# One weight queue over all projection parts, half-row norm steps, and output weights split on GpSimd in a one-core hybrid encoder layer

## The chip, the core and the metric

The kernel runs on one core of a Trainium2 chip. That core has a matrix engine (TensorE, in the profile PE for matmuls and PEld for weight loads), VectorE (DVE), ScalarE (ACT), GpSimd (POOL) and SyncE (SP), which here only issues DMAs. Data move between the chip's memory (HBM) and the on-chip buffers by 16 DMA engines, which the queues of SP and ACT feed. The metric is the device time of one execution in microseconds (us), lower is better.

## The reference, cut to what matters

One layer is run for 2048 prompt rows and for 8 streams of 16 sample rows (128 rows together), width 1024, all in float32:

```
n = rmsnorm(x)
z, xbc, dt_raw, q, k, v, f_raw = split_columns(n @ w_in)
y_ssd = ssd_mixer(z, xbc, dt_raw, ...)        # causal conv 4, chunked state scan, gate silu(z), group norm
y_fox = fox attention(q, k, v, cumsum(logf))  # 8 heads of 64, per-head forget gates, causal
h = x + concat(y_ssd, y_fox) @ w_out
u = causal_dwconv(rmsnorm(h) @ w_up)          # width 3
y = rmsnorm(h + (silu(u_gate) * u_value) @ w_down)
```

The outputs are y for both groups and the new caches and states.

## The kernel before, in words

Every float32 operand of a matmul is split into a high part (rounded) and a low part (the rest), and each product is three matmuls: high by high, high by low, low by high. The high part is made by a copy on ACT, the low part by a subtraction on POOL or DVE (`split`, `split2`).

The prompt is cut into four parts of 512 rows. Part 0 also holds the 128 sample rows (tile `SMP`). For each part, `a_head(p)` makes the normalised, transposed rows `nT`: it loads the transposed rows `xT`, finds the size of each row (`sizes` by plain rows `xt` on ACT, two half rows of 512 for each of four tiles, one `xt` buffer; for part 0 `sizes_by_columns` by matmul with ones), turns the sizes into diagonals `dg`, and multiplies. `a_body(p)` then projects: first v with the gate columns, v's other half, q and k, and after a break (`yield None`) the convolved x/B/C columns and z. `proj_tm` and `proj_cm` load their weight tile `craw` (two buffers) and split it into `cmw` (three buffers) where they are called. `gates(p)` turns the gate columns into decays and cumulative sums.

Attention (`attention`, in two passes: `s_phase` finds row maxima, `t_phase` the weights and sums) runs over the parts in order. Between its tiles the code places steps of the next projections by a credit (`fill`), and steps of a side job by a count (`sides`): `sample_attention` in part 0, the 17 SSD chunks (`ssd_chunk`) in parts 1 to 3. At attention tile 216 of 320 `out_steps` begins: `out_weights` loads and splits the eight rows of `w_out`, then `out_proj` computes `h` tile by tile, which goes on after attention. Last comes the ConvFFN over three groups of rows (`ffn_part`), untouched here.

The order of TensorE's instructions is the written one:

```
with tc.manual_schedule(engines={nc.tensor.engine}):
```

On ACT, DVE, POOL and SP a planner sets the order: it runs the program against a simulated clock and issues on each engine what is ready there, earliest written first. Each of these engines then runs its list in that order, whatever the real times are. A tile with `bufs=n` has n places; a new one waits until the last use of the one n before it. Four queue names pick the issuer of DMAs: `DQ = "sass"` makes `dma`, `dS` and `dA` go to SP and `dW` to ACT. Only weights (`dW`) are issued from ACT.

Of the kernel before, what the change touches and what calls it, by code (L numbers as in the profile page):

```python
# [17 lines left out]
P = 128  # L18
# [48 lines left out]
def hybrid_step(ctx: ExitStack, tc: tile.TileContext, i: dict, o: dict):  # L67
# [91 lines left out]
    def a_head(p):  # L159
# [18 lines left out]
        def sizes_by_columns(n, xTs):  # L178

            sq = at([P, 2, 4, 256], "cmw", WA)  # L180
            for kk in range(2):
                S.activation(sq[:, kk, :, :n * P], xTs[kk][:, :, :n * P], AF.Square)
            pz = tpt()
            for c in range(n):
                for k in range(KT):
                    T.matmul(pz[:, c:c + 1], sq[:, k // 4, k % 4, c * P:(c + 1) * P], ones[:, 0:1], start=k == 0, stop=k == KT - 1)
            ss = at([P, 2], "ss", 4)
            V.tensor_scalar(ss[:, 0:n], pz[:, 0:n], 1.0 / D, EPS, op0=ALU.mult, op1=ALU.add)
            G.tensor_tensor(ss[:, 0:n], ss[:, 0:n], mhalf[:, 0:n], op=ALU.pow)
            return [ss[:, c:c + 1] for c in range(n)]  # L190

        def sizes(c):
            ss = at([P, 2], "ss", 4)
            for hf in range(2):
                xt = at([P, 512], "xt", XB)
                dA(xt, i["xr"][c][:, hf * 512:(hf + 1) * 512])
                S.activation(xt, xt, AF.Square, accum_out=ss[:, hf:hf + 1])
            V.tensor_add(ss[:, 0:1], ss[:, 0:1], ss[:, 1:2])
            rsq(ss[:, 0:1], D)
            return ss[:, 0:1]  # L200

        def diagonals(ss):
            dgs = []
            for x in ss:
                dg = at([P, P], "dg", 2)
                S.activation(dg, ident, AF.Identity, scale=x)
                dgs.append(dg)
            return dgs

        def rows(e, w, c0, n, col, xsrc, xTs, dgs):  # L210
# [15 lines left out]
            for kk in range(0, KT, 4):  # L226
                xT = xTs[kk // 4]
                for k in range(4):
                    V.scalar_tensor_tensor(xT[:, k, :N], xT[:, k, :N], g1c[:, kk + k:kk + k + 1], pr[:, :N],
                                           op0=ALU.mult, op1=ALU.mult)  # L230
                split(xT[:, :, :N], wt[:, 0, kk:kk + 4, col:col + N], wt[:, 1, kk:kk + 4, col:col + N], S,
                      V if kk else G)
                if not kk:
                    yield

        if first:
            for t in todo:
                xTs = load(*t)
                dgs = diagonals(sizes_by_columns(t[3], xTs))
                yield  # L240
                for _ in rows(*t, xTs, dgs):
                    pass
                yield
# [13 lines left out]
    def gates(p, dtf):  # L257
# [11 lines left out]
        S.activation(u, u, AF.Exp, scale=-1.0)  # L269

# [5 lines left out]
        for m in (15, 13, 11, 9, 7, 5, 3):  # L276
            V.scalar_tensor_tensor(ac, ac, 1.0 / m, z, op0=ALU.add, op1=ALU.mult)
        V.scalar_tensor_tensor(ac, ac, 1.0, s, op0=ALU.add, op1=ALU.mult)
# [8 lines left out]
        if p == 0:  # L287
            dS(o["logf"][:, SMP], lf[:, 4])
        yield
# [17 lines left out]

        yield
# [68 lines left out]

    def a_body(p):
# [4 lines left out]
        def proj_tm(src, n, use):  # L383
            wm = []
            for e in range(2):
                raw = at([P, 4, 272], "craw", 2)
                dW(raw[:, :, :n], src[:, 4 * e:4 * e + 4])
                we = at([P, 2, 4, 272], "cmw", WA, F32R)
                split2(raw[:, :, :n], we[:, 0, :, :n], we[:, 1, :, :n], G)
                wm.append(we)  # L390
            for w, wt in wins:
                for c in win_tiles(w):
# [10 lines left out]
                    yield 1.45  # L403

# [19 lines left out]

        yield from proj_tm(i["w_tm0"], 272, use_v(1))
        gs = gates(p, dtf)
        next(gs)
        yield from proj_tm(i["w_tm"][0], 256, use_v(0))

        def load_cm(ct):  # L430
            raw = at([P, 4 * 272], "craw", 2)
            dW(raw[:, 0:D], i["w_cm"][ct])
            wc = at([P, 2, KT, P], "cmw", WA, F32R)
            split2(raw[:, 0:D].rearrange("p (k c) -> p k c", c=P), wc[:, 0], wc[:, 1], G)
            return wc

        def proj_cm(ct, use, pad):
            wc = load_cm(ct)
            for w, wt in wins:
# [10 lines left out]
                yield W * 0.0055  # L450

# [70 lines left out]
    def ssd_chunk(c):  # L522
# [6 lines left out]
        dma(sg.rearrange("p h l -> p (h l)"), ac_d[c:c + 1].rearrange("c h p -> c (h p)").to_broadcast([P, D]))  # L529

# [257 lines left out]
    def sample_attention():  # L788
# [33 lines left out]
        for b in range(NB):  # L822
# [11 lines left out]
            for a in range(2):  # L834
                vt = bt_([P, 2, 528], "k12", KB)
                dma(vt[:, :, 0:512], i["cv"][b, a * 256:(a + 1) * 256].rearrange("(c p) d -> p c d", p=P))
                vc += [vt[:, 0], vt[:, 1]]
            ps = [pss(), pss()]
# [49 lines left out]
    wo = []  # L888

    def out_weights():  # L890
# [19 lines left out]
    def out_proj(c, after=None):  # L910
        mr = op.tile([P, KT, P], F32, tag="raw", name="raw", bufs=2)
        mx = op.tile([P, 2, KT, P], F32R, tag="mx", name="mx", bufs=2)

        for ks in ([slice(0, KT - 1), slice(KT - 1, KT)] if 12 <= c < 16 else [slice(0, KT)]):
            dA(mr[:, ks], mix_d[c][:, ks])
            split(mr[:, ks], mx[:, 0, ks], mx[:, 1, ks], S, V)
# [10 lines left out]
        with tc.issue_after(after) if after is not None else ExitStack():  # L927
# [4 lines left out]
            else:  # L932
                for e in range(2):
                    for k in range(KT):
                        part(e, k)
                        if k % 2:
                            yield 1.36
        for e in range(2):
# [234 lines left out]
    def part_steps(p):  # L1173
# [3 lines left out]
        for k, c in enumerate(body):  # L1177
            if c is None:
                break
            if k in (12, 40) and hd:  # L1180
                next(hd)
# [16 lines left out]
    def out_steps():  # L1198
# [3 lines left out]
        for c in [SMP] + list(range(11)):  # L1202
            yield from out_proj(c)
# [4 lines left out]
    def open_out():  # L1208
# [9 lines left out]
    with tc.manual_schedule(engines={nc.tensor.engine}):  # L1218
        bodies = [a_body(0)]

        for k, c in enumerate(bodies[0]):
            if c is None:
                break
            if k < 4:
                next(head0)
            if k == 12:
# [6 lines left out]
        for u in att:  # L1233
# [20 lines left out]
            while gen is not None and credit > 0 and not hold:  # L1254
                c = next(gen, None)
                if c is None:
# [134 lines left out]
```

## Time and profile before

| | |
|---|---|
| median of 3 runs | 3159.74 us (3157.91 to 3166.94) |
| profiled execution | 3159.18 us, span of its instructions 3157.5 us |
| busy share of the span | PE 96%, PEld 85%, DVE 57%, ACT 34%, POOL 27% |
| mean granted TensorE clock | 0.984 of full |
| chain that ended last | PE 85%, DMA 8%, DVE 2%, ACT 2% |

A row of waits reads "who <- what ended the wait: us in total, times, longest". In a row of the time line, the bracket holds the idle time of the engine before the instruction and what ended it. PEclk is the granted clock of TensorE, 1.00 at 2.4 GHz and 0.50 at 1.2 GHz. ACTq and SPq are DMA issues and other work of these engines' sequencers.

### The profile page before, as it was taken

Reading aid. Unit: us, or ns where it says so; the run is one execution under the profiler, and the core shown is the slowest. Engines: PE = TensorE matmul, PEld = TensorE weight load, DVE = VectorE, ACT = ScalarE, POOL = GpSimd, SP = SyncE. Lnnn points to the kernel's source line nnn. Section 1 sums busy time; section 2 is a strip of 40 time slices with the busy share of each in tenths; the row PEclk is TensorE's granted clock in tenths of the full one; section 3 lists DMA queues with packets and bytes.
Section 4 is the critical chain, followed back from the end, with each engine's and each line's share of the span. In section 5 each row is a group of like instructions: output and inputs, shape, how many; then the busy total and the mean of one; then the engine's idle time right before and its main releaser. Section 6 shows DMA issues by size and latency. Waiting matters only on the chain.

```text
span 3157.5 us, 45849 instructions
## 1 busy us (share of the span) xinstructions
PE 3039.0 (96%) x17888; PEld 2682.1 (85%) x17888; DVE 1788.8 (57%) x3294; ACT 1066.7 (34%) x1927; POOL 865.8 (27%) x654
## 2 busy tenths in 40 slices
PE   7988998899999998999999999999999999999998
PEld 7886877787788775777899999999999999999998
DVE  4264466647565654543455555566555556766666
ACT  3343344444444444332322232233222223332322
POOL 3322322222222212000233232333223232433332
PEclk9998999899999999999999999999999999999999
DMA  4856675575556546445522121232121122322221
GB/s 123 247 174 202 200 244 158 181 223 165 162 155 204 153 132 187 161 148 181 171 67 67 54 69 61 72 116 79 61 67 61 60 67 83 105 67 81 74 69 65
DMA packets 233137, 395.77 MB, mean 125 GB/s; under 512 B 62544, under 2 KB 118488, under 8 KB 232920
## 3 DMA queue, kind: packets, MB, share of 16 engines
q1 hardware_dynamic: 181224, 238.41, 24.3%
q10 hardware_dynamic: 51696, 154.43, 15.8%
q8 instruction: 141, 2.31, 0.3%
q14 instruction: 76, 0.62, 0.1%
HBM read 314.51 MB, written 78.25 MB: 124 GB/s over the span
## 4 chain that ended last, share of the span: by engine, by line
PE 85%; DMA 8%; DVE 2%; ACT 2%; issue 1%; SPq 1%; POOL 1%; ACTq 0%; DVEq 0%; POOLq 0%
PE mm L120 11%; PE mm L121 11%; PE mm L122 11%; PE pv L696 6%; PE dn L1025 5%; PE dn L1026 5%; PE dn L1027 5%; PE mm L444 3%; PE mm L445 3%; PE mm L446 3%; DMA xt<-in_xr 2%; PE dn L923 2%; PE dn L925 2%; PE dn L924 2%; PE mm L397 2%; PE mm L399 2%
## 5 line engine op out<-in xcount | busy, mean ns | idle before, releaser
L105 POOL TENSOR_TENSOR wr<-raw,wr 128x1024 fp32r<-128x1024 f32 x198 | 476.5, 2415 | 1032.5 <-ACT wr L102 1024.5
L120 PE MATMUL mm<-nT,wr 128*128 128x386 f32 (+1 forms) x2112 | 696.4, 330 | 1.3 <-ACT wr L102 0.8
L121 PE MATMUL mm<-nT,wr 128*128 128x386 f32 (+1 forms) x2112 | 695.3, 329 | 0.1
L122 PE MATMUL mm<-nT,wr 128*128 128x386 f32 (+1 forms) x2112 | 694.4, 329 | 0.0
L1003 DVE SCALAR_TENSOR_TENSOR ac<-mm,cw,ac 128x384 f32<-128x384 f32 (+1 forms) x528 | 301.6, 571 | 344.8 <-ACT ac L1001 337.1
L1001 ACT ACTIVATE ac<-mm,cw 128x384 f32<-128x384 f32 (+1 forms) x264 | 172.7, 654 | 784.6 <-PE mm L122 784.0
L1028 DVE TENSOR_TENSOR y<-y,dn 128x512 f32<-128x512 f32 x374 | 255.0, 684 | 267.4 <-PE dn L1027 264.6
L121 PEld LDWEIGHTS mm<-nT,wr 128*128 128x128 f32 x2112 | 399.3, 189 | 6.8 <-DVE nT L105 0.3
L120 PEld LDWEIGHTS mm<-nT,wr 128*128 128x128 f32 x2112 | 397.5, 188 | 7.7 <-ACT wr L102 1.1
L122 PEld LDWEIGHTS mm<-nT,wr 128*128 128x128 f32 x2112 | 397.9, 188 | 5.7
L112 POOL TENSOR_TENSOR cmw<-craw,cmw 128x512 fp32r<-128x512 f32 (+1 forms) x192 | 248.6, 1317 | 467.8 <-ACT cmw L109 348.1
L444 PE MATMUL mm<-nT,cmw 128*128 128x256 f32 (+2 forms) x1024 | 309.7, 302 | 12.7 <-DVE cac L489 8.6
L671 DVE TENSOR_REDUCE nm<-s 128x1 f32<-128x512 f32 (+2 forms) x320 | 192.9, 607 | 198.6 <-PE s L668 114.1
L445 PE MATMUL mm<-nT,cmw 128*128 128x256 f32 (+2 forms) x1024 | 299.0, 292 | 0.0
L446 PE MATMUL mm<-nT,cmw 128*128 128x256 f32 (+2 forms) x1024 | 299.0, 292 | 0.0
L1025 PE MATMUL dn<-wr,ht 128*128 128x512 f32 x748 | 294.4, 394 | 2.9 <-DVE y L1028 1.7
L696 PE MATMUL pv<-pr,v 128*128 128x512 f32 (+3 forms) x640 | 293.5, 549 | 0.5 <-issue 0.5
L1026 PE MATMUL dn<-wr,ht 128*128 128x512 f32 x748 | 292.7, 391 | 0.0
L1027 PE MATMUL dn<-wr,ht 128*128 128x512 f32 x748 | 290.1, 391 | 0.0
L102 ACT CAST wr<-raw 128x1024 fp32r<-128x1024 f32 x198 | 203.2, 1042 | 174.1 <-PE dn L1027 161.4
L733 ACT ACTIVATE pr<-s 128x512 f32<-128x512 f32 (+1 forms) x320 | 169.3, 531 | 237.3 <-PE s L729 173.2
L668 PE MATMUL s<-ks,q 68*128 68x512 f32 (+2 forms) x320 | 199.8, 630 | 20.0 <-ACT pr L733 11.2
(294 smaller groups left out, 5174.9 us busy)
## 6 DMA issues: line engine op xcount, KB each, us to landing
raw<-in_w_up ACTq DMA_DIRECT2D x132, 512.0 KB
raw<-in_w_down ACTq DMA_DIRECT2D x66, 512.0 KB
craw<-in_w_cm ACTq DMA_DIRECT2D x64, 512.0 KB
k<-k_d SPq DMA_DIRECT2D x80, 256.0 KB
craw<-in_w_tm ACTq DMA_DIRECT2D x24, 512.0 KB
q_d<-qk SPq DMA_DIRECT2D x96, 128.0 KB
k_d<-qk SPq DMA_DIRECT2D x96, 128.0 KB
ks<-k_d SPq DMA_DIRECT2D x80, 136.0 KB
```

The costliest lines, as they stand in the source:

```text
L105: leng.tensor_sub(lo, src, hi.bitcast(F32))
L120: T.matmul(ps[:, :W], whi(k), wt[:, 0, k, :W], start=k == 0, stop=False)
L121: T.matmul(ps[:, :W], whi(k), wt[:, 1, k, :W], start=False, stop=False)
L122: T.matmul(ps[:, :W], wlo(k), wt[:, 0, k, :W], start=False, stop=k == n - 1)
L444: T.matmul(ps[:, :W], wc[:, 0, k, :], wk[:, 0], start=k == 0, stop=False)
L445: T.matmul(ps[:, :W], wc[:, 0, k, :], wk[:, 1], start=False, stop=False)
L446: T.matmul(ps[:, :W], wc[:, 1, k, :], wk[:, 0], start=False, stop=k == KT - 1)
L696: m = T.matmul(pv[:, of:512], vr[:, jj], pr[:, :512 - of], start=first, stop=last)
L1003: V.scalar_tensor_tensor(ac[:, 0:n], ps[:, j:j + n], cw2[:, ct, j:j + 1], ac[:, 0:n], op0=ALU.mult, op1=ALU.add)
L1025: T.matmul(ps, ht[:, 0, ts_], wd[:, 0, cc], start=x == 0, stop=False)
L1026: T.matmul(ps, ht[:, 0, ts_], wd[:, 1, cc], start=False, stop=False)
L1027: T.matmul(ps, ht[:, 1, ts_], wd[:, 0, cc], start=False, stop=x == len(g) - 1)
```

## The change

- The weight tiles of all four parts stand in one list (`wq`). `wload` issues the next raw tile from SP instead of ACT; `pump`, called at each projection step, splits the next loaded tile if one of the three `cmw` places is free and keeps two raw tiles ahead; `need` hands the tiles to the projections. The first two tiles are loaded and split inside `a_head(0)`.
- The order of the projections becomes v(second half), q0, v(first half), k0, q1, k1 ..., and after the break x0, z0, x1, z1, x2 to x7.
- `a_head(p)` for p > 0 issues one half row a step (calls at steps 8, 10, ..., 24 instead of all at step 12). The `xt` buffer is still one. For part 0 the squares move from `cmw` to the `k12` places, and the diagonals and the low parts go to DVE.
- `gates` has four more breaks and is advanced at each projection step instead of each projection.
- `ssd_chunk` has two more steps after its loads, `sample_attention` one more after its loads of each stream; one chunk moves from part 1 to part 2 and one more to part 3.
- `out_weights` splits wholly on POOL, without the `issue_after`; `out_rows` issues the load of the next tile's rows a tile ahead and splits them late in the tile before; three attention tiles pass between the first such load and its use.

```diff
         def sizes_by_columns(n, xTs):
-            sq = at([P, 2, 4, 256], "cmw", WA)
+            sq = []
             for kk in range(2):
-                S.activation(sq[:, kk, :, :n * P], xTs[kk][:, :, :n * P], AF.Square)
+                sq.append(bt_([P, 4 * 264], "k12", KB)[:, 0:D].rearrange("p (k t) -> p k t", k=4))
+                S.activation(sq[kk][:, :, :n * P], xTs[kk][:, :, :n * P], AF.Square)
...
-        def sizes(c):
-            ss = at([P, 2], "ss", 4)
-            for hf in range(2):
-                xt = at([P, 512], "xt", XB)
-                dA(xt, i["xr"][c][:, hf * 512:(hf + 1) * 512])
-                S.activation(xt, xt, AF.Square, accum_out=ss[:, hf:hf + 1])
-            V.tensor_add(ss[:, 0:1], ss[:, 0:1], ss[:, 1:2])
-            rsq(ss[:, 0:1], D)
-            return ss[:, 0:1]
+        def half_row(n):
+            xt = at([P, 512], "xt", XB)
+            dma(xt, i["xr"][todo[0][2] + n // 2][:, n % 2 * 512:(n % 2 + 1) * 512])
+            return xt
...
-                S.activation(dg, ident, AF.Identity, scale=x)
+                if first:
+                    V.tensor_scalar_mul(dg, ident, x)
+                else:
+                    S.activation(dg, ident, AF.Identity, scale=x)
...
-                      V if kk else G)
+                      V if kk or first else G)
...
-        ss = [sizes(todo[0][2] + c) for c in range(4)]
-        yield
+        xt = half_row(0)
+        yield
+        ss = []
+        for n in range(8):
+            if n % 2 == 0:
+                x = at([P, 2], "ss", 4)
+            S.activation(xt, xt, AF.Square, accum_out=x[:, n % 2:n % 2 + 1])
+            if n < 7:
+                xt = half_row(n + 1)
+            if n % 2:
+                V.tensor_add(x[:, 0:1], x[:, 0:1], x[:, 1:2])
+                rsq(x[:, 0:1], D)
+                ss.append(x[:, 0:1])
+            yield
...
+    def wload():
+        src, n = wq[len(raws)]
+        raw = at([P, 4 * 272], "craw", 2)
...
+        dma(raw, src.rearrange("p (k c) -> p k c", c=P) if n is None else src)
+        raws.append(raw)
+
+    def pump():
+        if len(tiles) < len(raws) and len(tiles) - used[0] < WA:
+            wsplit()
+        while len(raws) < len(wq) and len(raws) - len(tiles) < 2:
+            wload()
...
-        for pair in range(4):
-            for ct, kind in ((pair, 0), (4 + pair, 1)):
-                next(gs, None)
-                yield from proj_cm(ct, use_qk(kind, pair), 0)
+        for c in rest():
+            next(gs, None)
+            yield c
...
-        for ct in range(8):
-            yield from proj_cm(8 + ct, use_x(ct), PAD1)
-        yield from proj_tm(i["w_tm"][1], 256, use_z(0))
-        yield from proj_tm(i["w_tm"][2], 256, use_z(1))
+        yield from proj_cm(use_x(0), PAD1)
+        yield from proj_tm(256, use_z(0))
+        yield from proj_cm(use_x(1), PAD1)
+        yield from proj_tm(256, use_z(1))
+        for ct in range(2, 8):
+            yield from proj_cm(use_x(ct), PAD1)
...
-            with tc.issue_after(exps[-1]):
-                split2(raws[k], w[:, 0], w[:, 1], G)
+            split(raws[k], w[:, 0], w[:, 1], G, G)
...
-        for c in [SMP] + list(range(11)):
-            yield from out_proj(c)
+        cs = [SMP] + list(range(11))
+        g = out_rows(cs[0])
+        next(g)
+        yield ("wait", 3)
+        mx = next(g)
...
-    sides = {0: (sample_attention, 5 * NB + 1), 1: (lambda: chunks(SMP, 0, 1, 2), 49), 2: (lambda: chunks(3, 4, 5, 6, 7), 51),
-             3: (lambda: chunks(*range(8, 16)), 81)}
+    sides = {0: (sample_attention, 6 * NB + 1), 1: (lambda: chunks(SMP, 0, 1), 45), 2: (lambda: chunks(2, 3, 4, 5, 6), 61),
+             3: (lambda: chunks(*range(7, 16)), 109)}
```

## Rows read from the trace of the kernel before

**Rows 1.** Busy time in stretches of the span: the stretch and its length, then for each engine its busy time and instructions, then PEclk, the DMA engines' busy share and GB/s. 0 to 60 is the start, 140 to 600 holds the changes from part 0 to 1 and from 1 to 2, 1160 to 1260 the turn to the output projection, 1310 to the end mainly the ConvFFN.
```profile
0.00:60.00 60.00, 40.77 (x229) 39.61 (x229) 25.45 (x73) 20.56 (x29) 22.64 (x30) 0.97 0.36 116
140.00:260.00 120.00, 106.50 (x797) 97.26 (x798) 63.62 (x186) 44.60 (x98) 32.60 (x33) 0.97 0.59 186
260.00:360.00 100.00, 82.01 (x584) 65.70 (x583) 51.91 (x136) 37.05 (x84) 28.71 (x29) 0.81 0.63 192
460.00:600.00 140.00, 122.68 (x767) 101.71 (x766) 88.98 (x178) 53.66 (x114) 37.31 (x37) 0.93 0.58 176
600.00:1160.00 560.00, 547.58 (x3667) 449.59 (x3666) 332.51 (x643) 247.37 (x528) 146.72 (x156) 0.99 0.57 170
1160.00:1260.00 100.00, 82.09 (x390) 56.73 (x389) 49.01 (x77) 40.69 (x79) 26.41 (x30) 0.91 0.61 180
1310.00:3158.00 1848.00, 1833.01 (x9813) 1676.88 (x9811) 1070.01 (x1748) 541.67 (x817) 513.52 (x284) 1.00 0.27 86
```

**Rows 2.** Waits of TensorE's matmuls from 0 to 1310 us: who, what ended the wait, us in total, times, longest.
```profile
PE s L570 <- ACT pr L733: 12.6, 2, 9.1
PE s L668 <- ACT pr L733: 10.9, 5, 5.1
PE mm L444 <- DVE cac L489: 8.6, 3, 5.0
PE s L588 <- DVE ss L198: 7.8, 1, 7.8
PE tp L225 <- ACT dg L206: 7.7, 2, 5.8
...
PE s L668 <- DMA q<-q_d: 5.6, 2, 4.2
...
PE s L728 <- ACT pr L733: 4.4, 3, 2.1
...
PE tp L345 <- DVE g_2k L331: 1.6, 1, 1.6
```

**Rows 3.** Waits of ACT from 0 to 1310 us, same columns.
```profile
ACT xt L197 <- DMA xt<-in_xr: 64.7, 21, 6.3
...
ACT sg L532 <- DMA sg<-ac_d: 32.6, 12, 5.7
...
ACT wo L109 <- DMA raw<-in_w_out: 13.7, 3, 6.4
...
ACT cmw L182 <- PE tp L186: 10.2, 1, 10.2
```

**Rows 4.** Time line of the turn to the output projection, ACT and then TensorE: start, length, engine, line, instruction, tiles, shape, count, and the idle time before it.
```profile
1180.42 1.04 ACT L109 CAST wo<-raw 128x1024 fp32r<-128x1024 f32 x1 [5.79 <-DMA raw<-in_w_out]
...
1230.82 1.04 ACT L109 CAST wo<-raw 128x1024 fp32r<-128x1024 f32 x1 [6.43 <-DMA raw<-in_w_out]
1236.57 1.04 ACT L102 CAST mx<-raw 128x1024 fp32r<-128x1024 f32 x1 [4.71 <-DMA raw<-mix_d]
...
1182.02 0.80 PE L668 MATMUL s<-ks,q 68*128 68x512 f32 x1 [5.07 <-ACT pr L733]
...
1238.16 2.08 PE L570 MATMUL s<-sst,xb 128*128 128x256 f32 x4 [9.06 <-ACT pr L733]
```

**Rows 5.** Time line of the start, ACT, then POOL, then DVE, same columns.
```profile
16.39 2.00 ACT L182 ACTIVATE cmw<-qk 128x1024 f32<-128x1024 f32 x2 [5.40 <-DMA qk<-in_xTw]
...
19.56 0.69 ACT L206 ACTIVATE dg<-ident,ss 128x128 f32<-128x128 f32 x2 [1.17 <-DMA q_d<-q]
...
16.77 0.71 POOL L189 TENSOR_TENSOR ss<-ss,mhalf 128x2 f32<-128x2 f32 x1 [1.53 <-DVE ss L188]
24.09 2.35 POOL L105 TENSOR_TENSOR nT<-xT,nT 128x1024 fp32r<-128x1024 f32 x1 [6.61 <-ACT nT L102]
...
21.27 3.22 DVE L229 SCALAR_TENSOR_TENSOR xT<-xT,g1c,tp 128x256 f32<-128x256 f32 x8 [4.59 <-PE tp L225]
25.61 1.91 DVE L105 TENSOR_TENSOR nT<-xT,nT 128x1024 fp32r<-128x1024 f32 x1 [1.11 <-ACT nT L102]
```

**Rows 6.** All instructions of two lines of `a_head`: line, engine, instruction, count, duration in ns (least, median, most), start of the first and of the last in us, shape. The half-row squares of parts 1 to 3, and the diagonals made of the sizes.
```profile
L197 ACT ACTIVATE xt<-xt x24: 617/631/635, 113.6 to 569.9; 128x512 f32<-128x512 f32 x24
...
L206 ACT ACTIVATE dg<-ident,ss x17: 385/401/404, 19.6 to 852.0; 128x128 f32<-128x128 f32 x17
```

**Rows 7.** All weight loads of the projections, issued from ACT's sequencer (columns as in rows 6), and the longest sum of SP's own waits from 0 to 1310 us (the loads of attention's k).
```profile
L432 ACTq DMA_DIRECT2D craw<-in_w_cm x64: 334/335/382, 48.8 to 1060.5; - x64
...
L387 ACTq DMA_DIRECT2D craw<-in_w_tm x32: 347/385/453, 1.2 to 1109.3; - x32
...
SPq L623 <- PE s L729: 85.7, 31, 5.1
```

**Rows 8.** POOL: two groups by line and shape over the span (count, busy us, mean ns of one, idle before), and one row of its waits from 0 to 1310 us.
```profile
L636 POOL MEMSET v<- 128x256 f32 x80 | 24.9, 313 | 336.9 <-PE pv L696 259.3 <-issue 67.2 <-DMA h_d<-y 5.9
...
L112 POOL TENSOR_TENSOR wo<-raw,wo 128x512 fp32r<-128x512 f32 x16 | 20.2, 1282 | 24.8 <-ACT wo L109 24.3 <-DMA k<-k_d 0.4
...
POOL ss L115 <- DVE ss L198: 79.3, 11, 15.9
```

**Rows 9.** The low-part subtractions of `nT` on DVE before 1320 us (columns as in rows 6).
```profile
L105 DVE TENSOR_TENSOR nT<-xT,nT x8: 844/1222/2589, 25.6 to 875.7; 128x1024 fp32r<-128x1024 f32 x7, 128x512 fp32r<-128x512 f32 x1
```

More of the change, by code (lines that the diff above doesn't have):

```diff
@@ L185, in sizes_by_columns @@
                 for k in range(KT):
-                    T.matmul(pz[:, c:c + 1], sq[:, k // 4, k % 4, c * P:(c + 1) * P], ones[:, 0:1], start=k == 0, stop=k == KT - 1)
+                    T.matmul(pz[:, c:c + 1], sq[k // 4][:, k % 4, c * P:(c + 1) * P], ones[:, 0:1], start=k == 0, stop=k == KT - 1)
             ss = at([P, 2], "ss", 4)
@@ L376, in gates, with queue_of_weights, wsplit, need @@
         V.tensor_copy(nfs, pr[0:8, 0:256].rearrange("p (a t) -> p a t", a=2))
+    def queue_of_weights():
+        q = []
+        for p in range(NPART):
+            for x in ("v1", 0, "v0", 4, 1, 5, 2, 6, 3, 7, 8, "z0", 9, "z1", 10, 11, 12, 13, 14, 15):
+                if isinstance(x, int):
+                    q.append((i["w_cm"][x], None))
+                else:
+                    src, n = {"v1": (i["w_tm0"], 272), "v0": (i["w_tm"][0], 256), "z0": (i["w_tm"][1], 256),
+                              "z1": (i["w_tm"][2], 256)}[x]
+                    q += [(src[:, 4 * e:4 * e + 4], n) for e in range(2)]
+        return q
+    wq, raws, tiles, used = queue_of_weights(), [], [], [0]
+    def wload():
+        src, n = wq[len(raws)]
+        raw = at([P, 4 * 272], "craw", 2)
+        raw = raw[:, 0:D].rearrange("p (k c) -> p k c", c=P) if n is None else raw[:, 0:4 * n].rearrange("p (k c) -> p k c", c=n)
+        dma(raw, src.rearrange("p (k c) -> p k c", c=P) if n is None else src)
+        raws.append(raw)
+    def wsplit():
+        j = len(tiles)
+        n = wq[j][1]
+        if n is None:
+            we = at([P, 2, KT, P], "cmw", WA, F32R)
+        else:
+            we = at([P, 2, 4, n], "cmw", WA, F32R)
+        split2(raws[j], we[:, 0], we[:, 1], G)
+        tiles.append(we)
+    def pump():
+        if len(tiles) < len(raws) and len(tiles) - used[0] < WA:
+            wsplit()
+        while len(raws) < len(wq) and len(raws) - len(tiles) < 2:
+            wload()
+    def need(n):
+        while len(tiles) < used[0] + n:
+            if len(raws) == len(tiles):
+                wload()
+            wsplit()
+        return tiles[used[0]:used[0] + n]
     def a_body(p):
         wins = wins_of[p]
[L383 to L390, printed above, removed]
+        def proj_tm(n, use):
+            wm = need(2)
             for w, wt in wins:
@@ L423, in use_z, with proj_cm @@
             return f
[L425 to L438, printed above, removed]
+        def proj_cm(use, pad):
+            wc, = need(1)
             for w, wt in wins:
@@ L887, in hybrid_step @@
     tp = op = pso = None
-    wo = []
+    wo, ready = [], []
     def out_weights():
@@ L937, in out_proj @@
                             yield 1.36
+                        if e and k == 4 and nxt is not None:
+                            ready.append(next(nxt))
         for e in range(2):
@@ L1179, in part_steps @@
                 break
-            if k in (12, 40) and hd:
+            if hd and (k >= 8 and k % 2 == 0 and k <= 24 or k == 40):
                 next(hd)
@@ L1201, in out_steps @@
         yield from out_weights()
-        for c in [SMP] + list(range(11)):
-            yield from out_proj(c)
+        cs = [SMP] + list(range(11))
+        g = out_rows(cs[0])
+        next(g)
+        yield ("wait", 3)
+        mx = next(g)
+        for n, c in enumerate(cs):
+            g = out_rows(cs[n + 1]) if n + 1 < len(cs) else None
+            if g:
+                next(g)
+            yield from out_proj(c, None, mx, g)
+            mx = ready.pop() if g else None
     F = ExitStack()
```

45 lines of the change are left out of this document (40 added, 5 removed).

## The prediction, as it was put on record

> **What bounds the kernel now.** I read the stretches first. From 1310 us on TensorE is busy 1833 of 1848 us at full clock [rows 1]: that part is bound by its matmuls, and the diff leaves it alone. Between 600 and 1160 us only 12 of 560 us are idle. What can be won lies in four places: the start (19 of 60 us idle), 140 to 260 (13.5 us), 260 to 360 with 460 to 600 (18.0 and 17.3 us), and 1160 to 1260 (17.9 us). There the clock is low as well: a PEclk of 0.81 over 100 us is 38 us at the 1.2 GHz level, 0.93 over 140 us another 20, 0.91 over 100 us another 18. Each follows idle time of TensorE, and at the low level a busy TensorE loses at most half. The whole prize is some 85 us of idle time plus at most 40 us of clock. No matmul is removed, so everything below is about who makes TensorE wait.
>
> The waits of TensorE come next [rows 2]. They are nearly all for ACT: the exponentials (`L733`) or the diagonals. ACT is busy only about 40% in these stretches, so it isn't short of time; it stands. What it stands for is in its own waits [rows 3]: half rows `xt` 64.7 us, the broadcast `sg` 32.6 us, `w_out` tiles 13.7 us, and 10.2 us for one `cmw` place. ACT runs its list in order, so an exponential behind a copy that waits for a DMA waits too.
>
> **The change, part by part.**
>
> **Turn to the output projection.** The time line shows it without a guess [rows 4]: ACT stands 5.79 us for a `w_out` tile and TensorE has a gap of 5.07 us ending as that copy ends; then 6.43 us for the next late tile, directly followed by 4.71 us for the first row tile, and TensorE has a gap of 9.06 us. The change takes the `w_out` copies to POOL, so the first gap goes whole, and of the second the 6.43 us that came first. The row tile's own wait may stay: its copy is still on ACT, and three attention tiles more on TensorE don't move it in ACT's list. That is 5.1 + 6.4 = 11.5 of 17.9 us idle. Of the 9 us that the clock costs here at most, the same share is 5.8; part of the slow time is idle anyway, so I take 3.5. Together **−15 us** (bounds −18 and −5). POOL gets eight full-width copies. The trace has no such copy; the nearest rows are a memset of 256 columns at 0.31 us, thus 1.25 us for 1024 columns, and the subtraction at 2 × 1.28 us [rows 8]. With the subtraction a tile takes 3.8 to 5.1 us, all eight 30 to 41 us, in a stretch of 100 us where POOL is busy 26 [rows 1], 20 of them with these subtractions: hidden.
>
> **Start.** POOL has the first sizes at 16.77 + 0.71 = 17.48 us, ACT makes the diagonals at 19.56, behind two squares of the second window [rows 5]. On DVE, idle then, they come some 2 us sooner, and TensorE waits for exactly these (7.7 us in 2 waits [rows 2]). The second of those, 1.9 us, goes with the squares' new place: ACT stood 10.2 us for a `cmw` place. The low part on DVE instead of POOL gives nothing: the eight products end at 24.49, plus 1.91 is 26.40, where POOL ended at 26.44. **−4 us** (−6 to −2). The first weights now queue on SP behind the rows; they are needed at 24 us, so that is hidden.
>
> **Half rows.** This is the largest wait and the edit that aims at it, and I give it **0**. The planner does not wait for the place in the text: all 24 squares ran between 113.6 and 569.9 us, the diagonals of the last rows only at 852 [rows 6]. They are taken up as soon as a size place (four) and the one `xt` buffer are free. Both stay: the chain load, square, free, load has the same links, issued from the same queue. Only their rank among ready instructions drops, on an ACT with room to spare. If I am wrong and the waits vanish, the end is 18.0 us (260 to 360), the 7.8 us gap behind DVE's addition of the sizes [rows 2], and half of the 19 us of clock there: −35 us.
>
> **Weights from SP.** 64 issues at 0.335 and 32 at 0.385 us are 34 us of sequencer time [rows 7]. ACT loses them and gains nothing that TensorE sees, since it isn't short of time. SP gets them, and SP works in order and waits: behind a weight load that waits for POOL stand k, q, v, the half rows and all stores. POOL itself stood 79.3 us for sizes, up to 15.9 at once [rows 8], and the splits that free `craw` are queued behind. A late q cost TensorE 2.8 us apiece (5.6 in 2). I let two of the 96 loads do that: **+6 us** (0 to +60).
>
> **Order of the projections.** z among x spreads the convolution's load on DVE; TensorE waited 8.6 us on it. **−4 us** (−8.6 to +8, the loss being one gap like the 7.8 us one, since x6 and x7 now end a part, just before the next part's rows).
>
> **Steps.** The two steps after a chunk's loads don't touch ACT's wait for `sg`: its place is freed by the same matmul, and the planner puts the ACT work where the simulated load lands. Of the 4.4 us and 3.5 us that TensorE lost in this way, **−2 us** (−8 to 0). The sample step lies ahead of the first matmul of a stream, and the waits are mostly later: **−1 us** (−7 to 0). Gates, advanced sooner: 0, ends ±3, twice the one gate wait of 1.6 us. The moved chunks change nothing in sum.
>
> **Sum:** −15 − 4 + 0 + 6 − 4 − 2 − 1 = −20 us against the profiled execution of 3159.2 us (span 3157.5; 0.6 us under the median of the runs): **3139 us**.
>
> **The rivals.**
>
> *The half rows do come off the path.* For it: the wait is real and largest. Against: rows 6. 3139 − 35 = **3104 us**.
>
> *The stall changes engine.* Instead of ACT, POOL stands for the `w_out` tiles, and behind its copy stands the memset of a `v` place, without which SP may not load v. Then the 15 us return as late v and the start's 4 alone are kept with little else: 3139 + 15 + 4 = **3158 us**, no change. For it: POOL had 24.3 us of waits at this place already [rows 8]. Against: three v places.
>
> *DVE and POOL block each other.* The same subtraction on DVE took 844 to 2589 ns [rows 9], so something holds it at times. If each new POOL copy held DVE for its 2.4 us, 8 × 2.4 = 19 us would be lost: 3158 us. It needs DVE to be short of time, and it is busy 49 of 100 us there [rows 1]. The Trainium skill, SBUF — State Buffer, section "Who interferes with whom", says that a DVE instruction with two SBUF inputs and a GpSimd instruction that reads SBUF exclude each other for their whole length. The spread of rows 9 agrees with that rule but does not prove it; by the rule the loss is these 19 us if nothing covers them.
>
> *SP becomes the queue that everything stands in.* One place, the wait for a `craw` buffer at the head of SP's list, at 2.8 us apiece: without my 6 us the sum is 3133, so from 6 of the 96 loads on the gain is under 0.3%, from 13 on the kernel is slower by over 0.3%; at one in five, 20 loads, 3133 + 56 = **3189 us**. For it: SP already waits 85.7 us for k's places alone [rows 7], and POOL's 79 us. Against: 96 loads between 1.2 and 1109 us are one in 11.5 us, so most find their buffer free.
>
> **How the numbers follow.** 0.3% (9.5 us) is about what a measurement of this kernel can tell from no change. Forecast 0.48, half rows 0.18, the two rivals at 3158 us 0.17 together (the blocking one 0.04), SP 0.17. Faster: 0.48 + 0.18 = 0.66; same 0.17; slower 0.17. The forecast alone reaches from 3115 (the lower ends of output, start, order and steps, taken together in part) to 3150. The range of 3085 to 3176 takes in the half rows with a favourable remainder and the milder cases of SP; outside are 0.04 below and some 0.13 above.
>
> **What the profile after would show.** Right: no ACT wait of a `w_out` copy and no gap of over 5 us near 1177; ACT's wait for `xt` still above 45 us; first projection near 22 us instead of 24; the PE idle of 1160 to 1260 under 8 us. Wrong: ACT's wait for `xt` below 20 us (then the half rows were the larger part and the time is near 3100), or SP waits for POOL's `cmw` line of tens of us together with TensorE waiting for DMAs of k, q or v (then slower). That the planner's simulated clock deals the whole order anew is what could make single terms miss by their size.

## The result and the profile after

The changed kernel takes **3172.5 us** (median of 8 runs, 3169.3 to 3176.5) against 3160.4 us before (8 runs): ratio 1.0043, 95% interval 1.0032 to 1.0054. It became 12 us slower where 20 us less were forecast. The profiled execution has a span of 3169.1 us.

The stretches after, columns as in [rows 1] (the five engines are PE, PEld, DVE, ACT and POOL, in this order):

```profile
0.00:60.00 60.00, 41.62 (x250) 40.72 (x251) 32.61 (x84) 20.20 (x27) 20.07 (x29) 1.00 0.38 124
60.00:140.00 80.00, 72.93 (x485) 71.80 (x484) 21.61 (x73) 21.65 (x53) 21.77 (x20) 0.91 0.70 210
140.00:260.00 120.00, 109.10 (x834) 100.59 (x833) 64.56 (x179) 45.04 (x96) 36.32 (x35) 0.99 0.60 186
260.00:360.00 100.00, 76.89 (x590) 63.81 (x590) 52.78 (x145) 36.75 (x84) 26.11 (x27) 0.86 0.62 190
360.00:460.00 100.00, 91.35 (x792) 76.97 (x792) 42.45 (x110) 34.34 (x75) 26.47 (x23) 0.95 0.79 242
460.00:600.00 140.00, 125.58 (x765) 103.00 (x764) 89.41 (x178) 55.55 (x115) 32.20 (x33) 0.91 0.56 170
1160.00:1260.00 100.00, 83.48 (x384) 54.54 (x383) 62.84 (x94) 36.99 (x79) 35.41 (x32) 0.91 0.60 188
1310.00:3169.00 1859.00, 1843.37 (x9880) 1684.89 (x9878) 1078.36 (x1761) 546.64 (x831) 514.88 (x287) 1.00 0.27 86
```

Two stretches that I had not listed among the places with idle time have lost. These are the same two in the kernel before:

```profile
60.00:140.00 80.00, 76.33 (x541) 74.02 (x540) 25.41 (x78) 22.91 (x56) 26.09 (x23) 1.00 0.74 218
360.00:460.00 100.00, 98.06 (x878) 84.25 (x877) 54.61 (x134) 39.80 (x86) 27.86 (x25) 1.00 0.84 255
```

TensorE was idle 3.7 and 1.9 us there and ran at the 2.4 GHz level throughout; now it is idle 7.1 and 8.7 us, and part of the time it runs at the 1.2 GHz level. A third stretch lost idle time too, one that I had counted on: from 260 to 360 us it is idle 23.1 us after 18.0, though at a granted clock of 0.86 after 0.81. The turn to the output projection, 1160 to 1260, is about as idle as it was (16.5 against 17.9 us). What TensorE waits for, columns as in [rows 2]:

```profile
PE s L643 <- POOL xe L627: 7.9, 2, 5.2
...
PE tp L313 <- DVE g_ld L304: 7.3, 2, 4.5
...
PE mm L461 <- ACT nT L102: 6.0, 1, 6.0
...
PE s L798 <- DMA k<-k_d: 4.7, 2, 4.0
...
PE tp L383 <- DVE g_2k L104: 4.0, 1, 4.0
```

`g_ld` and `g_2k` belong to the gates; in the kernel before, this transpose waited 1.6 us for `g_2k` [rows 2], and nothing waited for `g_ld`. The waits of ACT, of POOL and of SP from 0 to 1330 us:

```profile
ACT xt L259 <- DMA xt<-in_xr: 60.8, 20, 8.7
...
ACT sg L602 <- DMA sg<-ac_d: 50.1, 12, 11.4
...
POOL wo L104 <- DMA raw<-in_w_out: 26.5, 5, 8.6
...
SPq L421 <- POOL cmw L112: 48.6, 31, 3.0
```

ACT no longer waits for `w_out`, POOL does, and for twice as long as ACT in [rows 3]. The half rows are waited for as before. ACT's waits for the broadcast `sg` grew, from 32.6 us [rows 3] to 50.1.

### The profile page after: what moved, and what is told of

It reads as the page before. It is cut to its first block, busy times and chain, and to the rows that moved or that the text cites. A ratio compares the mean times of both kernels' runs of the same rounds, so it can differ in the third digit from the quotient of the medians.

```text
span 3169.1 us, 45928 instructions
## 1 busy us (share of the span) xinstructions
PE 3043.2 (96%) x17888; PEld 2684.4 (85%) x17888; DVE 1793.7 (57%) x3302; ACT 1059.6 (33%) x1914; POOL 866.4 (27%) x651
## 4 chain that ended last, share of the span: by engine, by line
PE 83%; DMA 5%; DVE 2%; ACT 2%; issue 1%; SPq 0%; POOL 0%; DVEq 0%; POOLq 0%; ACTq 0%
PE mm L120 11%; PE mm L121 11%; PE mm L122 11%; PE pv L766 6%; PE dn L1108 5%; PE dn L1109 5%; PE dn L1110 5%; PE mm L497 3%; PE mm L498 3%; PE mm L499 3%; PE dn L1004 2%; PE dn L1006 2%; PE dn L1005 2%; PE s L799 2%; PE s L798 2%; PE s L738 2%
## 5 line engine op out<-in xcount | busy, mean ns | idle before, releaser
L497 PE MATMUL mm<-nT,cmw 128*128 128x256 f32 (+2 forms) x1024 | 304.4, 297 | 3.8 <-ACT ev L518 3.1
L498 PE MATMUL mm<-nT,cmw 128*128 128x256 f32 (+2 forms) x1024 | 296.2, 289 | 0.0
L499 PE MATMUL mm<-nT,cmw 128*128 128x256 f32 (+2 forms) x1024 | 295.9, 289 | 0.0
```

Of the source, the lines that this page charges most:

```text
L497: T.matmul(ps[:, :W], wc[:, 0, k, :], wk[:, 0], start=k == 0, stop=False)
L498: T.matmul(ps[:, :W], wc[:, 0, k, :], wk[:, 1], start=False, stop=False)
L499: T.matmul(ps[:, :W], wc[:, 1, k, :], wk[:, 0], start=False, stop=k == KT - 1)
```

## The experiments

Every ratio is to the kernel before, on the same chip in the same rounds; differences between kernels are taken between ratios, times 3160 us. "Gates old" is an edit that runs through several kernels: the added pauses in `gates` are gone, and one step stands ahead of each projection.

**How much is noise.** The control moves a write that should be worth nothing:

```
-            if k == 12:
+            if k == 16:
                 constant_rows()
```

> A control: the changed kernel with the constant rows written four half projections later, an edit that should be worth nothing by itself. It shows how much the time moves when the planner deals the order of instructions anew. If single parts own the loss: within 2 us of the changed kernel, 3170 to 3175. If the order as such is worth several us: it moves by 4 us or more, in either direction, and differences of that size between the other kernels say nothing of their edits.

Ratio 1.0059 (1.0044 to 1.0074), 3178.8 us: 5 us more than the changed kernel. The intervals overlap, so even these 5 us are not shown to be more than noise. A difference of about 5 us between two of these kernels says nothing of its edit.

**Five parts undone one at a time.** Gates:

```
-        for c in rest():
-            next(gs, None)
-            yield c
+        next(gs)
+        yield from proj_cm(use_qk(0, 0), 0)
+        next(gs, None)
+        yield from proj_tm(256, use_v(0))
+        next(gs, None)
+        yield from proj_cm(use_qk(1, 0), 0)
...
```

> The changed kernel with the gates as before: one step of the gates before each projection instead of one at every half projection, and none of the added pauses inside them. Theory A (the gates now put TensorE in front of chains on DVE): the loss of 60 to 140 us goes (TensorE busy there about 76 instead of 73 us, granted clock 1.00 instead of 0.91), the wait of TensorE for g_ld (7.3 us) and for g_2k (4.0 us) shrinks to under 3 us together, and the time falls by some 8 to 12 us, to 3160 to 3164. Theory B (the gates are covered; the loss lies in the weights' queue or in the steps): within 3 us of the changed kernel, 3169 to 3176.

Output weights:

```
-            split(raws[k], w[:, 0], w[:, 1], G, G)
+            with tc.issue_after(exps[-1]):
+                split2(raws[k], w[:, 0], w[:, 1], G)
```

> The changed kernel with the output weights' high parts copied by ACT again, behind the last exponential, and only the low parts on GpSimd. My prediction's step (the copies on ACT cost 15 us): slower by 5 to 18 us than the changed kernel, 3178 to 3190, with ACT waiting for w_out again. The rival (the stall changes engine: xe on GpSimd now stands behind the copies, TensorE waits 7.9 us for it): within 4 us of the changed kernel, 3168 to 3176; the waits for xe go, those for the copies come back.

Weights' queue: `dma(raw, ...)` in `wload` becomes `dW(raw, ...)`, so these loads are issued from ACT again.

> The changed kernel with the weights' loads issued from ACT's queue again, all else as changed. If SP's waits for the raw weight places (48.6 us for GpSimd's low parts, 17.2 us for ACT's copies) hold back the loads of k, q and the cache: the waits of TensorE for DMAs of k, v and ckT (4.7, 3.2, 3.9 us) go and the time falls by 6 to 12 us, to 3160 to 3166. If these waits are covered: within 3 us, 3169 to 3176. If ACT's own list then stands for the places instead: slower, up to 3185.

Steps: the two pauses behind a chunk's loads, the one behind a sample stream's loads, and the `sides` as before.

> The changed kernel without the added pauses in the chunks and the sample attention, with the chunks dealt to the parts as before. If the pauses and the moved chunks make the loss of 360 to 460 us (TensorE busy 91.4 instead of 98.1 us there, clock 0.95 instead of 1.00): that stretch is whole again and the time falls by 5 to 12 us, to 3160 to 3167. If they gain what I forecast: slower by 1 to 5 us, 3173 to 3178. If no single part owns the loss because every edit deals the order anew: a move of some us with no relation to that stretch.

Sizes: no pause between half rows, one step as before.

> The changed kernel with the row sizes of a part in one step again, at the places where the kernel before had them. My prediction's step (half rows worth nothing, since the planner hoists them and the chain with one buffer stays): within 3 us of the changed kernel, 3169 to 3176, ACT's wait for xt again 55 to 70 us. If the half rows crowd SP and DMA in 320 to 460 us (where TensorE lost some 12 us): that stretch is whole again (under 3 us idle in 400 to 460, granted clock 1.00) and the time falls to 3158 to 3164. If they come off the path and gain: slower by 10 us or more.

| undone | ratio | 95% | against the changed kernel |
|---|---|---|---|
| gates | 1.0061 | 1.0048 to 1.0075 | +6 us |
| output weights | 1.0040 | 1.0026 to 1.0054 | -1 us |
| weights' queue | 1.0049 | 1.0037 to 1.0062 | +2 us |
| steps | 1.0049 | 1.0035 to 1.0063 | +2 us |
| sizes | 1.0055 | 1.0040 to 1.0070 | +4 us |

None of the five gives the loss back, and none differs from the control beyond the intervals. So none of them, undone alone, is the cause; a cause that two edits share would not show here.

**The order of the projections.** The old order, and then the old order with the gates old:

```
-  "v1", 0, "v0", 4, 1, 5, 2, 6, 3, 7, 8, "z0", 9, "z1", 10, 11, 12, 13, 14, 15
+  "v1", "v0", 0, 4, 1, 5, 2, 6, 3, 7, 8, 9, 10, 11, 12, 13, 14, 15, "z0", "z1"
```

> The changed kernel with the old order of the projections (v before q; z after all of x). Theory A (the new order is the loss: q in place of v behind the first projection gives the gates' chain on DVE 5 us of cover instead of 14, and z among x puts its loads where the DMA engines are full): the waits for g_ld (2.8 and 4.5 us) shrink, 400 to 460 us is whole again (clock 1.00 instead of 0.91), and the time falls by 8 to 13 us, to 3160 to 3165. Theory B (gates alone, whatever the order): the wait for g_ld stays, since with a step at every half projection the matmul comes as soon as before: within 3 us, 3169 to 3176. My forecast (the order gains 4 us): slower, 3175 to 3178.

> The changed kernel with both, the old order and the old steps of the gates. If order and gates only hurt together (a matmul of the gates ahead of its chain on DVE): no wait of TensorE for the gates over 2 us, the stretch of 60 to 140 us busy 76 instead of 73 us at clock 1.00, and the time lower than with the old order alone by 4 us or more, near 3158. If the order alone is the cause: the same as with the old order alone within 3 us. If neither is: 3169 to 3176.

Old order: 0.9982 (0.9971 to 0.9992), 3153.7 us, 19 us less than the changed kernel. With the gates old as well: **0.9960 (0.9948 to 0.9973), 3148.2 us**, 26 us less. This version beats both kernels. The two stretches that I had not listed, in this version:

```profile
60.00:140.00 80.00, 77.25 (x542) 75.15 (x541) 23.97 (x77) 24.53 (x60) 25.60 (x23) 1.00 0.74 218
...
360.00:460.00 100.00, 91.02 (x761) 76.66 (x760) 50.86 (x125) 37.22 (x80) 25.73 (x23) 0.97 0.75 227
```

60 to 140 us is whole again, 360 to 460 is not. The order's two halves one at a time, v before q (z still among x), and z last (q still before v):

> The changed kernel with v before q again behind the first projection, z still among x. The old order as a whole was worth 19 us (3172 to 3154). Theory V (most of it is the cover of the gates' chain at the start of a part: five v tiles instead of one q): 3154 to 3160, and TensorE's wait for g_ld at some 327 us (4.5 us) falls to under 2 us. Theory Z (most is z among x: x2 to x7 on DVE and the loads of the next part's rows fall together, and z's weights meet the stores of k in 400 to 420 us): 3167 to 3173, with the gap of 3.4 us at 414 us left.

> The changed kernel with z after all of x again, q still before v. Theory V: within 4 us of the changed kernel, 3168 to 3176, with the g_ld wait of 4.5 us at some 327 us still there. Theory Z: 3154 to 3161, with the gaps at 414 us (3.4 us), 431 us (2.7 us) and 863 us (3.9 us) smaller. If both matter and add up, this and the kernel before share the 19 us; if they share less than 12 or more than 26, the order dealt anew is part of it.

v before q: 1.0047 (1.0032 to 1.0062), +1 us. z last: 1.0002 (0.9987 to 1.0016), -13 us. Alone, the first is worth nothing; behind z last it is worth 6 us (1.0002 to 0.9982), near the noise.

And the new order by itself, in the kernel before (there the weights' loads move with it):

> The kernel before with nothing but the new order of the projections (q before v, z among x; its weights still from ACT's queue, its gates one step before each projection). If the order costs by itself what it costs in the changed kernel: slower by 13 to 24 us than before, 3172 to 3184. If it costs only together with the other edits (the weights loaded ahead, the half rows): within 5 us of before, 3155 to 3165. My forecast for the order: 4 us faster, 3156.

1.0041 (1.0027 to 1.0055), 3172.5 us: by itself the order costs the kernel before 13 us. No other edit is needed for the loss. (Its two halves were not run apart in that kernel.) What it does there shows in the waits of TensorE:

```profile
PE tp L291 <- DVE dt_t L302: 8.3, 1, 8.3
...
PE tp L291 <- DVE g_ld L283: 6.3, 2, 4.3
```

and in the time line of DVE at the start of part 1 in the same kernel:

```profile
324.79 0.17 DVE L413 COPY dtf<-mm 128x16 f32<-128x16 f32 x1 [1.04 <-ACT ev L410]
...
331.19 3.69 DVE L277 SCALAR_TENSOR_TENSOR g_a<-g_a,g_z 128x64 f32<-128x64 f32 x7
...
335.75 0.17 DVE L283 TENSOR_SCALAR g_ld<-g_t 128x32 f32<-128x32 f32 x1
```

From the last column of `dtf` to `g_ld` the gates' chain takes 335.9 - 324.8 = 11.1 us. The matmul that needs `g_ld` stands in TensorE's fixed list behind one projection. With q there, TensorE has nothing left to do 2.9 us after that last column and stands for 8.3 us (the profile names `dt_t`, which DVE copies just behind `g_ld`). The kernel before has v at this place, DVE and then TensorE:

```profile
320.89 0.17 DVE L413 COPY dtf<-mm 128x16 f32<-128x16 f32 x1 [1.04 <-ACT ev L410]
...
329.50 0.17 DVE L283 TENSOR_SCALAR g_ld<-g_t 128x32 f32<-128x32 f32 x1
...
333.92 0.33 PE L291 MATMUL tp<-g_ld,tri 128*128 128x64 f32 x2
```

The chain takes 8.8 us there, v covers 13.0 us, and the matmul starts without a wait.

**What z among x does on DVE.** The stretch of 230 to 280 us, the end of part 0, first the changed kernel, then the one with z last:

```profile
230.00:280.00 50.00, 37.43 (x286) 31.44 (x285) 36.18 (x98) 22.07 (x47) 14.01 (x13) 0.90 0.59 187
```

```profile
230.00:280.00 50.00, 39.23 (x316) 32.13 (x312) 21.52 (x61) 19.02 (x43) 14.70 (x14) 0.86 0.66 201
```

With x2 to x7 at the end, DVE (the third engine) is busy 36 instead of 22 of 50 us just when the next part's rows come to it. TensorE is busy 37.4 and 39.2 us, so this stretch by itself accounts for 1.8 us. At the end of part 2 the changed kernel shows what is late, DVE first and TensorE below:

```profile
860.88 2.43 DVE L228 SCALAR_TENSOR_TENSOR xT<-xT,g1c,tp 128x256 f32<-128x256 f32 x6
863.23 0.68 DVE L669 TENSOR_TENSOR yt<-yt,xd 128x512 f32<-128x512 f32 x1
863.83 0.86 DVE L228 SCALAR_TENSOR_TENSOR xT<-xT,g1c,tp 128x256 f32<-128x256 f32 x2
864.61 1.78 DVE L552 SCALAR_TENSOR_TENSOR cth<-cth,cac 128x256 f32<-128x256 f32 x1
866.43 0.69 DVE L756 CAST q<-s 4x512 fp32r<-4x512 f32 x1
...
867.17 0.50 PE L799 MATMUL s<-q,k 68*128 68x512 f32 x1 [3.87 <-DVE q L756]
```

The row products and the convolution's last product `cth` stand ahead of the copy into q that attention waits for. To test it, only z's second half goes behind x again:

```
-  "z0", 9, "z1", 10, 11, 12, 13, 14, 15
+  "z0", 9, 10, 11, 12, 13, 14, 15, "z1"
```

> The changed kernel with only z's second half behind all of x again (z's first half among x, q before v as changed). Theory D (the loss is DVE at the end of a part: x2 to x7 each give it three multiply-adds and a product just when the next part's rows come; DVE is busy 36 of 50 us in 230 to 280 us with z among x and 22 with z last): one half of z behind x is cover enough, 3159 to 3165, and the 3.9 us wait of TensorE for DVE's q at some 863 us goes. Theory S (the loss is where z's weights and stores meet the stores of k, at the front): half or none of it returns, 3167 to 3174, and the gap at 414 us stays above 3 us.

1.0014 (1.0001 to 1.0026), 3164.9 us: 9 of the 13 us come back. DVE is busy 28.6 of the 50 us, and the 3.87 us gap is down to 0.82:

```profile
865.11 0.49 PE L798 MATMUL s<-q,k 68*128 68x512 f32 x1 [0.82 <-DVE q L755]
```

The gap that begins at 414 us stayed (3.4 us in the changed kernel, 3.6 here), so the front of z is not what was gained. That speaks for DVE at a part's end. It doesn't prove it: the single gaps do not add up to the whole 9 us, and the kernel before, with z last, also has a gap of TensorE for the copy into q there (2.43 us).

**The turn to the output projection**, four kernels on top of the old order with the gates old (3148 us). `xe` of chunks 10 to 15 on DVE:

```
-        G.tensor_mul(h3(xe), h3(xd), b8(te[:, c]))
+        (V if 10 <= c < 16 else G).tensor_mul(h3(xe), h3(xd), b8(te[:, c]))
```

> The old order and the old gate steps (3148 us) with xe of chunks 10 to 15 on DVE instead of GpSimd, so that it no longer stands behind the copies of the output weights. If that standing is what became of the 15 us forecast at the turn: TensorE's waits for xe (6.1 us in 1160 to 1260) vanish, 1160 to 1260 us idle falls from 19 to under 13 us, the time by 5 to 9 us to 3139 to 3143. If another wait (the diagonal, the sg broadcast on ACT) takes its place: idle there stays above 16 us, the time within 3 us of 3148.

Six raw tiles of `w_out` loaded ahead (tiles 2 to 5 lie in the two `mx` places):

```
-        load(0)
-        load(1)
+        for k in range(6):
+            load(k)
```

> The old order and the old gate steps (3148 us) with six raw output weight tiles loaded ahead instead of two (the places of the row tiles are used for them). If GpSimd's standing for the late w_out transfers (16.6 us in 1160 to 1260) is the stall: it falls below 5 us, the waits of TensorE for xe with it, and the time falls by 4 to 8 us. If more loads at once only crowd the transfers of q, k and sg: idle there stays above 16 us and ACT's wait for sg (18.2 us) grows; the time within 3 us of 3148 or above.

Half the pace: `yield ("wait", 2)` becomes `yield ("wait", 4)`.

> The old order and the old gate steps (3148 us) with the output weights taken up half as fast: four attention tiles between two of them instead of two. Six tiles loaded ahead made it 10 us slower. If the transfers of w_out crowd those of sg, q and k at the turn: TensorE's idle time in 1140 to 1260 us falls from 19 to under 13 us, ACT's wait for sg from 18 to under 10 us, the time by 4 to 8 us. If the chain of a chunk itself (sg, sum, diagonal of sizes) sets the gaps: idle above 16 us, the time within 4 us of 3148.

A small broadcast, with `xe` on DVE: for the same chunks (`few`) it loads one head of `sg` instead of eight and uses it for all, so what it computes for these chunks leaves out seven heads:

```
+            dma(sg[:, 0], ac_d[c:c + 1, 0].to_broadcast([P, P]))
-            S.activation(sg[:, h], sg[:, h], AF.Relu, scale=-1.0, bias=acs[:, c, h:h + 1])
+            S.activation(sg[:, 7 - h], sg[:, 0 if few else 7 - h], AF.Relu, scale=-1.0, bias=acs[:, c, 7 - h:8 - h])
```

> The old order, the old gate steps and xe of chunks 10 to 15 on DVE (3147 us), and the broadcast sg of these chunks loads one head (64 KB) instead of eight (512 KB) and uses it for all eight: the outputs of these chunks are left wrong, the instructions on the engines are the same. If what is left of the stall at the turn is ACT standing for sg's transfer (8.8 us, with a 6.1 us gap of TensorE behind it): the wait falls below 3 us, TensorE's idle time in 1140 to 1260 us from 18 to under 12 us, the time by 4 to 9 us to 3138 to 3143. If the next link of the chunk (its sizes on GpSimd and its diagonal product yt on DVE, a gap of 4.9 us) takes its place: idle stays above 15 us, the time within 3 us of 3147.

| kernel | ratio | 95% | TensorE idle, 1160 to 1260 us |
|---|---|---|---|
| base | 0.9960 | 0.9948 to 0.9973 | 19.2 us |
| `xe` on DVE | 0.9960 | 0.9947 to 0.9973 | 18.2 us |
| six tiles ahead | 0.9997 | 0.9983 to 1.0010 | 21.4 us |
| half the pace | 0.9985 | 0.9970 to 1.0000 | 22.0 us |
| small broadcast | 0.9985 | 0.9976 to 0.9994 | 19.9 us |

With `xe` on DVE the wait for `xe` that the edit reaches went, and a longer one came behind ACT's `sg` (6.1 us after 2.4). The wait for `xe` that is left (3.5 us) belongs to the chunk just before, whose `xe` this edit leaves on POOL:

```profile
PE pv L756 <- ACT pr L793: 6.1, 1, 6.1
PE s L673 <- DVE yt L669: 4.9, 1, 4.9
PE s L633 <- POOL xe L617: 3.5, 1, 3.5
...
1166.92 1.24 POOL L617 TENSOR_TENSOR xe<-xd,te 128x512 f32<-128x512 f32 x1
```

So moving every `xe` of this stretch was not tried.

The small broadcast didn't take that wait away either. SP and then ACT in its time line:

```profile
1194.84 0.49 SPq L961 DMA_DIRECT2D raw<-in_w_out  x1
1197.36 0.45 SPq L961 DMA_DIRECT2D raw<-in_w_out  x1
1201.27 0.34 SPq L589 DMA_DIRECT2D sg<-ac_d  x1
...
1209.82 2.15 ACT L596 ACTIVATE sg<-sg,acs 128x128 f32<-128x128 f32 x7 [7.23 <-DMA sg<-ac_d]
...
1253.92 0.33 SPq L589 DMA_DIRECT2D sg<-ac_d  x1
...
1256.94 2.15 ACT L596 ACTIVATE sg<-sg,acs 128x128 f32<-128x128 f32 x7 [3.15 <-PE s L634]
```

64 KB issued at 1201.27 let ACT go only at 1209.82, 8.5 us later, behind two `w_out` tiles of 512 KB issued 4 to 6 us earlier and some loads of k and v. ACT took up its `sg` work 7 us too soon once more. The next broadcast, issued at 1253.92 with no `w_out` on the way, was there within 3.0 us. That points to what else is being loaded, not to the size of `sg`; no run isolates it. Neither the engine of the copies nor the size of `sg` is the one cause, and `xe` of the later chunks isn't either; the chunk's chain meets the next late link each time. Which edit would shorten the chain itself stays open, and so does why the last three are slower than their base (for the small broadcast, `xe` on DVE; by 8 us, which neither expectation had).

## Why the prediction was wrong, point by point

**Order of the projections: -4, bounds -8.6 to +8; measured +13 alone and +19 in the changed kernel.** This is the step that failed. I put the spread of the convolution's load on DVE into the sum as a gain, and the crowded end of a part only into the bound, as "one gap like the 7.8 us one". The gain is there but small: TensorE's waits for `cac` are 0.5 us in the changed kernel and 1.0 us with z last. The loss is larger than the bound: z behind x again gives 13 us back. I looked only at z, counted one end of a part where there are three, and put q in place of v at nothing without a reason. Its cost could be read before: a chain on DVE of 8.8 us from `dtf` to `g_ld`, set against the length of the projection ahead of its matmul. What q in place of v costs in time is less clear than its gap of 8.3 us: 1 us with z among x, 6 us with z last.

**Gates: 0, ends +-3.** With the new order, undoing the steps did nothing for TensorE in 60 to 140 us (busy 72.9 of 80 us, as in the changed kernel). With the steps, undoing the whole order did nothing there either (72.4). With both undone it is 77.3 us. Two edits take the same cover away, so in this stretch each looks innocent when it alone is undone. In the whole time the gates are worth 7 us once the order is old (0.9982 to 0.9960), with intervals that just overlap. I had priced them from a wait of 1.6 us that was short because of that cover.

**Turn to the output projection: -15, bounds -18 to -5; measured none.** TensorE's idle time went from 17.9 to 16.5 us, and giving the copies back to ACT changed nothing (-1 us). The copies cost a little less than I said (1.04 us undisturbed, against 1.25). The failing step is "hidden": I set POOL's busy time against its free time, and forgot that POOL also works in order and would stand for the late transfers, with its copies and subtractions bunched up behind them. The rival in which the stall changes engine was right, through `xe` and not through v. (Its 3158 us were added up wrongly: with the start's 4 us alone kept it is 3155.) The rows:

```profile
1214.39 1.04 POOL L104 CAST wo<-raw 128x1024 fp32r<-128x1024 f32 x1 [6.73 <-DMA raw<-in_w_out]
1219.35 1.52 POOL L104 CAST wo<-raw 128x1024 fp32r<-128x1024 f32 x1 [3.92 <-DMA raw<-in_w_out]
...
1223.38 1.03 POOL L627 TENSOR_TENSOR xe<-xd,te 128x512 f32<-128x512 f32 x1
...
1224.47 2.07 PE L643 MATMUL s<-xe,bs 128*128 128x256 f32 x4 [5.23 <-POOL xe L627]
```

That is the changed kernel, POOL and then TensorE: two waits for `w_out`, `xe` behind them and behind a copy and a subtraction, TensorE's gap of 5.23 us ending with `xe`.

The rival that DVE and POOL block each other also came in part. DVE's `yt` took 2.1 us both times in 1160 to 1260, beside a subtraction of POOL, against 0.68 both times in the kernel before and in the one with the copies back on ACT. First POOL and DVE after, then DVE before:

```profile
1224.38 2.34 POOL L105 TENSOR_TENSOR wo<-raw,wo 128x1024 fp32r<-128x1024 f32 x1
1225.17 2.10 DVE L669 TENSOR_TENSOR yt<-yt,xd 128x512 f32<-128x512 f32 x1
...
1242.59 0.68 DVE L599 TENSOR_TENSOR yt<-yt,xd 128x512 f32<-128x512 f32 x1
```

This is a step of the same chunk chain. It is not new with the change: two instructions of DVE's L609 took 2.86 us together beside a subtraction in the kernel before. I had priced the rival at 2.4 us for each copy, where a copy takes 1.04 us and the held instruction lost 1.4 beside a subtraction. What it cost in time is not isolated.

**Start: -4; TensorE's idle time fell by 0.9 us (60 less the busy time of [rows 1]), and the first projection comes at 24.24 us, after 24.06 before, not 22.** The diagonals came 3 us sooner, where some 2 were forecast. Then ACT gave the gain away:

```profile
16.67 0.48 DVE L203 TENSOR_SCALAR dg<-ident,ss 128x128 f32<-128x128 f32 x2 [0.83 <-POOL ss L190]
18.27 3.22 DVE L228 SCALAR_TENSOR_TENSOR xT<-xT,g1c,tp 128x256 f32<-128x256 f32 x8 [1.12 <-PE tp L224]
...
22.20 1.04 ACT L109 CAST cmw<-craw 128x1024 fp32r<-128x1024 f32 x1 [6.02 <-DMA craw<-in_w_cm]
23.15 1.99 ACT L102 CAST nT<-xT 128x1024 fp32r<-128x1024 f32 x2
...
24.24 0.59 PE L461 MATMUL mm<-cmw,nT 128*128 128x272 f32 x1 [6.01 <-ACT nT L102]
```

The row products end at 21.49, but ACT stands until 22.20 for a weight tile that is used later, and copies it first. I had looked only at when the first weights are needed, not at what is queued behind the copy of the third. The step that failed is again "hidden", here of the first weights on SP. Right behind these lines DVE's two subtractions took 3.67 us, 1.8 apiece, beside POOL's own of the weights, against a middle value of 1.22 in [rows 9]. The Trainium skill, SBUF — State Buffer, section "Who interferes with whom", has such pairs exclude each other; this agrees with it, and no run isolates it.

**Half rows: 0; right.** ACT waits 60.8 us for `xt` after 64.7, and undoing the part changed +4 us, within the noise. **Weights from SP: +6; none shown.** The sign I gave for it came, SP's 48.6 us for POOL's `cmw` beside 7.9 us of TensorE's waits for k, but with the weights on ACT's queue again the time was +2 us; so the sign was no proof of the cause. **Chunk and sample steps: -3; none shown** (+2 us undone). **The rival of SP as one queue** did not come.

**The rest of the sum.** With order and gates undone the other edits together give 13 us (interval 8 to 16) where their terms made -16. I don't count that as right: the two terms that carried it, turn and start, are not where it is. So of the 33 us between the forecast of 3139 and the 3172 measured, 30 are order with gates (-4 forecast, +26 measured) and 3 the rest. About half of what the rest gives is idle time saved in 600 to 1160 us (5.7 instead of 12.4 us), which I had left out; which edit does that is open, since no single undoing differed from the control.

**The signs.** Right: no ACT wait for a `w_out` copy, `xt` still above 45 us. Wrong: the first projection near 22, and idle under 8 us at the turn.

## What to carry to other kernels

Where one engine runs a fixed list, price a new order by chains: for each step that another engine prepares, set the length of that chain (here 9 to 11 us) against what now stands between, and do it for every repetition. Moving a copy that waits for a transfer to another in-order engine can move the stall to whatever is queued behind it there; compare waits, not busy shares. When two edits remove the same cover, undoing one shows nothing, so undo them in pairs, and run a neutral edit first to know which differences the runs can tell.

## What the runs showed that I had not expected

A write moved by four half projections came out 5 us slower, too little to tell from noise, but as much as most single edits here. A transfer's size hardly counted at the turn: an eighth of the bytes still took 8.5 us from issue to use, against 10.1 us for the whole. A DVE instruction of 0.68 us took 2.1 us beside a subtraction on POOL. More loads ahead made the kernel slower, by 12 us for six tiles instead of two (0.9997 against 0.9960), with TensorE's granted clock in 1160 to 1260 us down from 0.91 to 0.85.
